# Attention's output products as three matmuls of 64 columns into one set of bank columns, instead of 128 and 64 columns and a sum

## The chip, the cores and the metric

The kernel runs on one core of a Trainium2 chip. The core has a matrix engine (TensorE, called PE in the rows), a vector engine (VectorE, DVE), an activation engine (ScalarE, ACT), a general engine (GpSimd, POOL) and a queue for transfers (SyncE, SP). PE reads its operands from on-chip memory and writes into eight accumulation banks of 512 float32 columns by 128 partitions, from which DVE and ACT read. The metric is the device time of one execution in microseconds; a number for a kernel is the median of its runs.

## What is computed

The reference is two layers of a backbone over 1024 latent tokens and 256 context tokens with 1024 features: normalise and modulate, one input projection, four parallel branches, an output projection and a gated residual. Two of the four branches are attention, over all keys (type C) and over a window (type D), and for both the part that matters here is

```
s = jnp.einsum('bgrid,bgjd->bgrij', q_blk, k, preferred_element_type=jnp.float32) * ATTN_SCALE
p = jax.nn.softmax(s, axis=-1).astype(v.dtype)
return jnp.einsum('bgrij,bgjd->bgrid', p, v)
```

with heads of 64 features, two heads of queries for each head of keys and values, and blocks of 128 query rows. The last line, probabilities times values, is what the change rewrites.

## The kernel before

Float32 products are made out of shorter numbers. For the projections (`unit_a` L429 and `unit_b` L443) a weight and an activation are each split in a high and a low part and three of the four cross products are summed in a bank. For attention, probabilities and values are split into float16 high and low parts: H and L of the probabilities P, transposed by DMA into one tile PT that holds all high tiles and then all low ones, and `vh`, whose columns 0 to 63 hold the high values of a head and 64 to 127 the low ones.

A job of attention is a block of 128 query rows with one head of type C over its ten key tiles, or two heads of type D over up to five each. It runs through a chain of steps: `scores` (PE fills up to three banks S, L974), `largest` (DVE finds the row maxima and copies S into P, L993 to L1006), `exp` (ACT, L1015), `high` (ACT makes H, L1023), `low` (DVE and POOL make L, L1032; both are transposed by DMA into PT), `values` (PE, L1045, into a bank O), `out` (ACT copies the first 64 columns of each head from O into M, L1057) and `add` (DVE adds the other 64 columns to M, L1061, and gives the bank O back). When all jobs of a chunk have been added, `norm` divides M by the sums, `turn` transposes it on PE and `gate` (DVE, L1090) multiplies with the gate.

In `values` each key tile of a head has a product of the high probabilities with all 128 columns of `vh`, and one of the low probabilities with its first 64 columns. So the bank's first 64 columns get two of the three cross products and its second 64 the third, which is why a sum of two parts follows.

The order on every engine is written by a planner at build time. It keeps a rough clock of each engine: a matmul of n columns of float16 is put down as the larger of 30 and 0.425 n ns, an operation of DVE as 130 + 1.2 n ns. Steps of jobs are queued with the time at which they are due, and `hook`, which is called between the matmuls of the projections, runs those that are due. A new job's scores are started when fewer than three jobs are in flight, enough of the six banks of tag `pm` (S, O and other small results share them) are free, and DVE and ACT are not too far behind. At the end of a group that needs the memory of attention the planner lets PE stand until the jobs are through.

Of the kernel before, what the change touches and what calls it, by code (L numbers as in the profile page):

```python
# [16 lines left out]
AF = mybir.ActivationFunctionType  # L17
# [173 lines left out]
class Program:  # L191
# [766 lines left out]
    def scores(self, typ, p, qk, vh, inv, t, t0, n, box, heads, keys, masks):  # L958
        V, S, G, T, SP = self.V, self.S, self.G, self.T, self.SP
        l, lc, nk = self.l, self.lc[self.l], len(keys)  # L960
        nh, ws, w = len(heads), 128 * nk, 128 * nk * len(heads)
        cols = [(s, kt) for s in range(nh) for kt in keys]
# [3 lines left out]
        for s in range(nh):  # L966
            i = 0
            while i < nk:
                o, m = s * nk + i, 1
                while i + m < nk and keys[i + m] == keys[i] + m and (o + m) % 4:  # L970
                    m += 1
                for b in (2, 3):
                    c = 128 * (o % 4)
# [52 lines left out]
        def low(P, H, L):  # L1026

            pt = self.tile(self.ap, (128, 20, 128), F16, "PT", "PT")
            SP.dma_start_transpose(out=pt[:, 0:w // 128, :], in_=H[:, 0:w])
            c = w * LOWS // 8  # L1030
            for E, a, b in ((V, 0, c), (G, c, w)):
                E.tensor_sub(L[:, a:b], P[:, a:b], H[:, a:b])  # L1032
            self.done(P)
            self.flight -= 1
            SP.dma_start_transpose(out=pt[:, w // 128:w // 64, :], in_=L[:, 0:w])
            self.done(H, L)
            self.pe(lambda: values(pt), "pm", lambda: vh() is not None)

        def values(pt):
            O = self.pm("O")  # L1040
            for j, (s, kt) in enumerate(cols):
                for pl in range(2):

                    m = 128 - 64 * pl
                    T.matmul(O[:, 128 * s:128 * s + m], pt[:, pl * len(cols) + j, :], vh()[:, kt, 0:m],  # L1045
                             start=(j % nk == 0 and pl == 0), stop=(j % nk == nk - 1 and pl == 1))
            self.done(pt)
            box["over"]("values")
            self.later(lambda: out(O), "", lambda: "M" in box or self.has("M"))

        def out(O):
            if "M" not in box:
                box["M"] = self.tile(self.gp, (128, 512), F32, "M", "M")
            M, c = box["M"], 128 * (t - t0) + 64 * heads[0]
            ov = O[:, :128 * nh].rearrange("p (h s d) -> p h s d", h=nh, s=2)
            mv = M[:, c:c + 64 * nh].rearrange("p (h d) -> p h d", h=nh)
            S.activation(mv, ov[:, :, 0, :], AF.Copy)  # L1057
            self.later(lambda: add(M, mv, ov, O))

        def add(M, mv, ov, O):  # L1060
            V.tensor_add(mv, mv, ov[:, :, 1, :])  # L1061
            self.done(O)
            box["left"] -= 1
            if box["left"] == 0:
                gi = 0 if typ == "C" else 1
                self.later(lambda: norm(M, gi), "gd smv", lambda: ("silu", l, gi, p, t0) in self.made)

        def norm(M, gi):
            gt = self.gd(n="gt")
            SP.dma_start(out=gt[:, :128 * n], in_=self.sgd[l][gi, p, :, 128 * t0:128 * (t0 + n)])  # L1070
            sv, rs = box["sum"], self.sm("v", "rs")
            if typ == "D":
                V.tensor_add(rs[:, 8:8 + 2 * n], sv[:, 0:2 * n], sv[:, 8:8 + 2 * n])
                V.reciprocal(rs[:, 0:2 * n], rs[:, 8:8 + 2 * n])
            else:
                V.reciprocal(rs[:, 0:2 * n], sv[:, 0:2 * n])
            m3 = M[:, :128 * n].rearrange("p (t d) -> p t d", d=64)
            self.e("msum").tensor_mul(m3, m3, rs[:, 0:2 * n].unsqueeze(2).to_broadcast([128, 2 * n, 64]))
            self.done(sv, rs)
            self.pe(lambda: turn(M, gt))  # L1080
# [714 lines left out]
```

## Time and profile before

| | |
|---|---|
| median of 3 runs | 1315.66 us (1308.14 to 1317.33) |
| the profiled execution | 1318.18 us |
| its span, first to last instruction | 1316.4 us |
| mean granted clock of TensorE | 0.987 |
| PE busy | 1272.4 us (97%) |
| DVE busy | 841.8 us (64%) |
| ACT busy | 703.4 us (53%) |
| POOL busy | 610.6 us (46%) |

Times in the rows are microseconds from the first instruction unless they are marked ns. L1045 is line 1045 of the kernel, `O<-vh,PT` means that O is written from vh and PT, and x20 that twenty instructions stand in the row. PEld is the loading of weights into the matrix engine, which can run beside its matmuls. A busy share of PE near one does not say that PE is at its peak: each matmul's recorded length contains a latency that overlaps the next one's, so the pitch at which matmuls start says more than their lengths. In the chain of work that ended last, a row is a start, a length and the work of that stretch. In the timeline, a row is a start, the time from the first start to the last end, and the instructions; in brackets stands for how long the engine had been idle before, and what it waited for. In the table by stage a row is a stretch, its length, and each engine's busy time in it, then the granted clock (1.00 is 2.4 GHz, 0.50 is 1.2 GHz), the share of DMA and GB/s.

### The profile page before, as it was taken

The numbers are of one execution on the slowest core, as the hardware profiler recorded it, in microseconds if no ns is written. First come the engines' busy times: TensorE is split into PE (matmuls) and PEld (weight loads), VectorE is DVE, ScalarE is ACT, GpSimd is POOL, SyncE is SP. The second block draws the span as 40 slices with busy tenths as digits, with TensorE's granted clock in tenths as the row PEclk, the third lists the DMA queues.
The fourth block names the chain that finished last, engine by engine and source line by source line (L and its number), as shares of the span: only waits on it lengthen the run. The fifth ranks groups of instructions, "written<-read, shape, count | busy, mean of one in ns | idle before, by whom it ended". The sixth has DMA issues, their size and how long they took to land.

```text
span 1316.4 us, 27946 instructions
## 1 busy us (share of the span) xinstructions
PE 1272.4 (97%) x10720; PEld 1121.9 (85%) x10720; DVE 841.8 (64%) x2022; ACT 703.4 (53%) x1467; POOL 610.6 (46%) x616
## 2 busy tenths in 40 slices
PE   6989999999999899999999999999999889999998
PEld 4877878889989788888999978789888778888998
DVE  4765878888897734237225957778898884523522
ACT  3555768777776831235224647667778674213210
POOL 2585855835843213234112486769486422323320
PEclk9999999999999999999999999999999999988999
DMA  9426899799789922163612257997988985105531
GB/s 365 151 77 153 136 203 214 145 201 204 146 164 192 213 75 69 45 190 115 216 33 99 90 142 145 193 196 134 189 170 156 198 162 117 40 21 196 181 112 49
DMA packets 373351, 194.13 MB, mean 147 GB/s; under 512 B 303297, under 2 KB 333665, under 8 KB 372193
## 3 DMA queue, kind: packets, MB, share of 16 engines
q1 hardware_dynamic: 373072, 192.28, 62.6%
q8 instruction: 84, 1.38, 0.4%
q14 instruction: 51, 0.41, 0.1%
q10 hardware_dynamic: 144, 0.07, 0.0%
HBM read 94.63 MB, written 23.74 MB: 90 GB/s over the span
## 4 chain that ended last, share of the span: by engine, by line
PE 79%; DVE 9%; POOL 3%; ACT 3%; issue 3%; DMA 3%; SPq 1%; POOLq 0%; ACTq 0%; DVEq 0%
PE ua L429 32%; PE ub L443 26%; PE S L974 6%; PE O L1045 5%; DVE P L993 2%; PE y L1418 2%; PE y L1414 2%; PE mod L520 1%; POOL rr L567 1%; DMA xt<-in_x 1%; PE u L1714 1%; PE kvp L1330 1%; PE sc L1386 1%; DVE qr L827 1%; DVE L L1032 1%
## 5 line engine op out<-in xcount | busy, mean ns | idle before, releaser
L429 PE MATMUL ua<-w,HT 128*128 128x256 f32 x4128 | 525.2, 285 | 0.4 <-ACT vt L1275 0.4
L429 PEld LDWEIGHTS ua<-w,HT 128*128 128x128 f32 x4128 | 502.8, 191 | 3.8 <-issue 1.7
L443 PE MATMUL ub<-HT,w 128*128 128x512 f32 (+1 forms) x1824 | 402.8, 374 | 4.8 <-ACT kT L1293 2.5
L443 PEld LDWEIGHTS ub<-HT,w 128*128 128x128 f32 x1824 | 311.7, 193 | 63.3 <-ACT kT L1293 3.3
L372 POOL TENSOR_TENSOR w<-raw,w 128x512 fp32r<-128x512 f32 x132 | 185.1, 1413 | 269.3 <-ACT w L370 240.2
L1032 DVE TENSOR_TENSOR L<-P,H 128x1120 f16<-128x1120 f32 (+2 forms) x104 | 143.1, 1376 | 18.2 <-ACT H L1023 16.8
L370 ACT ACTIVATE w<-raw 128x512 fp32r<-128x512 f32 x136 | 83.3, 625 | 109.1 <-PE ua L429 49.2
L993 DVE CUSTOM_DVE_ANT_0 P<-S,zero 128x512 f32<-128x512 f32 (+2 forms) x216 | 116.1, 581 | 29.7 <-PE S L974 14.0
L974 PE MATMUL S<-qkt 128*128 128x256 f16 (+2 forms) x768 | 124.7, 304 | 4.1 <-DVE mx L993 4.1
L1032 POOL TENSOR_TENSOR L<-P,H 128x160 f16<-128x160 f32 (+2 forms) x104 | 81.3, 782 | 97.2 <-ACT H L1023 65.0
L1023 ACT ACTIVATE H<-P 128x1280 f16<-128x1280 f32 (+2 forms) x104 | 124.5, 1197 | 2.1 <-DMA PT<-H 1.2
L1015 ACT ACTIVATE P<-P,mx,gmxC 128x1280 f32<-128x1280 f32 (+1 forms) x72 | 97.5, 1354 | 17.7 <-DVE mx L1002 16.6
L1045 PE MATMUL O<-vh,PT 128*128 128x128 f16 (+1 forms) x1952 | 101.8, 207 | 4.3 <-DVE M L1061 3.1
L974 PEld LDWEIGHTS <-qkt 128*128 128x128 f16 x768 | 64.5, 98 | 45.5 <-issue 7.6
L1045 PEld LDWEIGHTS <-PT 128*128 128x128 f16 x1952 | 88.2, 98 | 14.4 <-issue 8.0
L1598 DVE TENSOR_TENSOR tm<-ua,gb 128x512 f32<-128x512 f32 (+1 forms) x37 | 24.9, 674 | 114.5 <-PE ua L429 114.5
L573 ACT ACTIVATE ev<-ub 128x512 f32<-128x512 f32 (+1 forms) x64 | 34.7, 542 | 110.0 <-PE ub L443 89.7
L567 POOL TENSOR_TENSOR rr<-rt,mhalf 128x6 f32<-128x6 f32 (+3 forms) x60 | 76.2, 1269 | 5.0
L1015 ACT ACTIVATE P<-P,mx,gmxD 128x640 f32<-128x640 f32 (+2 forms) x72 | 61.4, 853 | 16.9 <-DVE mx L1006 12.5
L1121 DVE SCALAR_TENSOR_TENSOR sl<-th,ev 128x512 f32<-128x512 f32 (+1 forms) x40 | 34.4, 860 | 34.5 <-ACT th L1116 32.9
L993 DVE CUSTOM_DVE_ANT_0 P<-S,mask 128x512 f32<-128x512 f32 (+2 forms) x112 | 50.5, 483 | 8.1 <-PE S L974 5.4
L827 POOL TENSOR_TENSOR rt<-sw,cst 128x192 f32<-128x192 f32 x64 | 49.2, 789 | 3.0 <-ACT sw L833 2.6
(177 smaller groups left out, 1547.0 us busy)
## 6 DMA issues: line engine op xcount, KB each, us to landing
raw<-in_win SPq DMA_DIRECT2D x104, 256.0 KB
raw<-in_wmod SPq DMA_DIRECT2D x64, 256.0 KB
wm<-in_wmod SPq DMA_DIRECT2D x8, 1024.0 KB
raw<-in_wout SPq DMA_DIRECT2D x32, 256.0 KB
xt<-in_x SPq DMA_DIRECT2D x4, 1024.0 KB
silu<-sl SPq DMA_DIRECT2D x16, 256.0 KB
gt<-silu SPq DMA_DIRECT2D x16, 256.0 KB
mxd<-mg SPq DMA_DIRECT2D x16, 256.0 KB
```

The costliest lines, as they stand in the source:

```text
L370: self.S.activation(w[:, :, 0, :], rv, AF.Copy)
L372: self.e(f"w{'i' if o < 0 else 'to'[o > 0]}low{q}").tensor_sub(w[:, :, 1, :], rv, w[:, :, 0, :].bitcast(F32))
L429: self.T.matmul(ps[:, 256 * i:256 * i + 256], self.HT[:, 2 * pair + i, k, sa, :], W[k // 2][:, k % 2, sb, :], start=(j == 0 and n == 0), s ...
L443: self.T.matmul(ps[:, :128 * n], W[k // 2][:, k % 2, sa, 128 * b:128 * b + 128], self.HT[:, t0:t0 + n, k, sb, :], start=(k == 0 and m == 0 ...
L567: self.G.tensor_tensor(r[:, :n], t[:, :n], self.mhalf[:, :n], ALU.pow)
L827: E.tensor_mul(out[:, :, :, 32 * c:32 * c + 32], x[:, :, :, 32 * c:32 * c + 32], t.to_broadcast([128, 2, 3, 32]))
L974: T.matmul(sp[o // 4][:, c:c + 128 * m], qk[:, t, heads[s], :], qk[:, keys[i]:keys[i] + m, b, :], start=(b == 2), stop=(b == 3))
L993: V.tensor_tensor_reduce(out=P[:, 128 * o:128 * (o + m)], in0=sp[o // 4][:, c:c + 128 * m], in1=mk, scale=1.0, scalar=-3e38, op0=ALU.add, ...
L1015: S.activation(P[:, ws * s:ws * s + ws], P[:, ws * s:ws * s + ws], AF.Exp, scale=lc["c"][typ][0], bias=mx[:, s:s + 1], accum_out=sv[:, col ...
L1023: S.activation(H[:, 0:w], P[:, 0:w], AF.Copy)
L1032: E.tensor_sub(L[:, a:b], P[:, a:b], H[:, a:b])
L1045: T.matmul(O[:, 128 * s:128 * s + m], pt[:, pl * len(cols) + j, :], vh()[:, kt, 0:m], start=(j % nk == 0 and pl == 0), stop=(j % nk == nk ...
```

## The change

`values` makes the three cross products as three matmuls of 64 columns. All three go into the same 64 columns of the bank, so the bank sums them. The high probabilities are the weights of the first two, which read the high and the low values; the low probabilities are those of the third. A weight load stands ahead of every matmul, before and now. `out` copies the finished columns, 64 for each head and next to each other, and gives the bank back. The step `add` with its instruction of DVE is gone, and what it did besides (it counts the jobs that are left and starts `norm`) is now done by `out`.

```
-                for pl in range(2):
-
-                    m = 128 - 64 * pl
-                    T.matmul(O[:, 128 * s:128 * s + m], pt[:, pl * len(cols) + j, :], vh()[:, kt, 0:m],
-                             start=(j % nk == 0 and pl == 0), stop=(j % nk == nk - 1 and pl == 1))
+
+                for pl, pv in ((0, 0), (0, 1), (1, 0)):
+                    T.matmul(O[:, 64 * s:64 * s + 64], pt[:, pl * len(cols) + j, :], vh()[:, kt, 64 * pv:64 * pv + 64],
+                             start=(j % nk == 0 and pl + pv == 0), stop=(j % nk == nk - 1 and pl == 1))
...
-            ov = O[:, :128 * nh].rearrange("p (h s d) -> p h s d", h=nh, s=2)
-            mv = M[:, c:c + 64 * nh].rearrange("p (h d) -> p h d", h=nh)
-            S.activation(mv, ov[:, :, 0, :], AF.Copy)
-            self.later(lambda: add(M, mv, ov, O))
-
-        def add(M, mv, ov, O):
-            V.tensor_add(mv, mv, ov[:, :, 1, :])
+            S.activation(M[:, c:c + 64 * nh], O[:, :64 * nh], AF.Copy)
             self.done(O)
```

The planner's clocks see other lengths, so it deals the rows of attention out anew. On PE, the start of the first output block was this before (ua is a projection's bank, O_1536 the output bank):

```order
L429 MATMUL ua_1475<-w_1207,HT 128x256 x6
L1045 LDWEIGHTS PT_1404
L1045 MATMUL O_1536<-vh_993,PT_1404 128x128
L1045 LDWEIGHTS PT_1404
L1045 MATMUL O_1536<-vh_993,PT_1404 128x64
```

and is this now, where the matmul stands on line 1044:

```order
L429 MATMUL ua_1475<-w_1207,HT 128x256 x6
L1044 LDWEIGHTS PT_1404
L1044 MATMUL O_1536<-vh_993,PT_1404 128x64
L1044 LDWEIGHTS PT_1404
L1044 MATMUL O_1536<-vh_993,PT_1404 128x64
L1044 LDWEIGHTS PT_1404
L1044 MATMUL O_1536<-vh_993,PT_1404 128x64
```

A key tile's two loads and two matmuls have become three and three; the program has 976 more of each on PE.

On DVE, late in the second layer's attention, the row of the maxima of one job (L1006) was followed by an add and the next subtraction before:

```order
L1006 TENSOR_SCALAR mx_14617<-mx_14617 128x2
L1061 TENSOR_TENSOR M_14370<-M_14370,O_14577 128x128
L1032 TENSOR_TENSOR L_14635<-P_14499,H_14634 128x1120
L1073 TENSOR_TENSOR rs_14676<-sum_14145 128x8
L1074 RECIPROCAL rs_14676<-rs_14676 128x8
L703 TENSOR_SCALAR tb_14683<-tab_14594,lconst_9554 128x128
```

and is now followed by the reciprocals of a chunk that is complete, and then the subtraction:

```order
L1006 TENSOR_SCALAR mx_15430<-mx_15430 128x2
L1066 TENSOR_TENSOR rs_15453<-sum_14928 128x8
L1067 RECIPROCAL rs_15453<-rs_15453 128x8
L1032 TENSOR_TENSOR L_15449<-P_15309,H_15448 128x1120
L703 TENSOR_SCALAR tb_15509<-tab_15426,lconst_10002 128x128
```

The add has left DVE's queue there, as it has in 104 places, and the reciprocals moved ahead of the subtraction.

On PE, shortly behind that place, two pieces of a projection (ub) stood ahead of two jobs' scores in a row before; the rows are the end of the projection, and the start of the first job's scores:

```order
L579 MATMUL mt_14812<-cst,M_14370 128x128 x4
L443 MATMUL ub_14774<-HT,w_14014 128x256 x6
L443 MATMUL ub_14774<-HT,w_14570 128x256 x6
L974 LDWEIGHTS qkt_13547
L974 MATMUL S_14852<-qkt_13547 128x256
```

Now one job's scores stand ahead of those two pieces, and the other's behind them; the rows are the end of the first job's scores, the projection, and the start of the second job's:

```order
L974 LDWEIGHTS qkt_14238
L974 MATMUL S_15653<-qkt_14238 128x256
L443 MATMUL ub_15592<-HT,w_14646 128x256 x6
L443 MATMUL ub_15592<-HT,w_15382 128x256 x6
L974 LDWEIGHTS qkt_14238
L974 MATMUL S_15703<-qkt_14238 128x256
```

One of the two jobs moved ahead of 12 matmuls of the projection.

## Rows read from the trace of the kernel before

**Rows 1.** The page: busy time, share of the span, instructions of PE and DVE

```profile
PE 1272.4 (97%) x10720; PEld 1121.9 (85%) x10720; DVE 841.8 (64%) x2022; ACT 703.4 (53%) x1467; POOL 610.6 (46%) x616
```

**Rows 2.** The page: the chain that ended last, shares of the span by engine

```profile
PE 79%; DVE 9%; POOL 3%; ACT 3%; issue 3%; DMA 3%; SPq 1%; POOLq 0%; ACTq 0%; DVEq 0%
```

**Rows 3.** Busy time by stage: the two layers' attention

```profile
90.00:500.00 410.00, 400.92 (x3675) 348.08 (x3674) 316.59 (x858) 279.22 (x571) 217.47 (x229) 0.99 0.84 168
...
800.00:1110.00 310.00, 300.00 (x2765) 260.45 (x2763) 249.09 (x677) 222.22 (x434) 180.23 (x185) 0.99 0.86 167
```

**Rows 4.** Groups by line and form: products and adds (busy us, mean ns; idle before)

```profile
L1045 PE MATMUL O<-vh,PT 128*128 128x128 f16 x976 | 98.6, 221 | 3.7 <-DVE M L1061 3.1 <-DVE mx L993 0.6
L1045 PE MATMUL O<-vh,PT 128*128 128x64 f16 x976 | 94.5, 193 | 0.6 <-DMA PT<-L 0.5
...
L1061 DVE TENSOR_TENSOR M<-M,O 128x64 f32<-128x64 f32 x64 | 13.4, 210 | 1.4 <-ACT M L1057 1.3
...
L1061 DVE TENSOR_TENSOR M<-M,O 128x128 f32<-128x128 f32 x40 | 11.1, 280 | 19.1 <-ACT M L1057 19.1
```

**Rows 5.** Timeline of PE and PEld, one output block and what follows it

```profile
154.22 1.02 PE L1045 MATMUL O<-vh,PT 128*128 128x128 f16 x20
...
154.22 0.88 PEld L1045 LDWEIGHTS <-PT 128*128 128x128 f16 x20
...
155.06 0.19 PE L1045 MATMUL O<-vh,PT 128*128 128x64 f16 x1
155.08 0.38 PE L974 MATMUL S<-qkt 128*128 128x512 f16 x1
```

**Rows 6.** The chain from 150 to 165 us: an output and a score block

```profile
154.38 0.87 PE O L1045 x20
155.25 1.08 PE S L974 x6
```

**Rows 7.** The bank O: idle time before its instructions until (us, times)

```profile
  ACT M L1057: 20.4, 12
  DVE M L1061: 3.1, 2
```

**Rows 8.** Timeline of ACT, then of DVE, in stretch B

```profile
1029.43 0.45 ACT L1057 ACTIVATE M<-O 128x128 f32<-128x128 f32 x2 [0.36 <-POOL ge L1250]
...
1031.04 1.33 DVE L1032 TENSOR_TENSOR L<-P,H 128x1120 f16<-128x1120 f32 x1
1032.28 0.48 DVE L1061 TENSOR_TENSOR M<-M,O 128x128 f32<-128x128 f32 x2
```

**Rows 9.** Timeline of PE: a wait in B, a projection ahead of C

```profile
1032.61 1.01 PE L1045 MATMUL O<-vh,PT 128*128 128x128 f16 x20 [1.64 <-DVE M L1061]
...
1070.93 1.68 PE L443 MATMUL ub<-HT,w 128*128 128x256 f32 x12
```

**Rows 10.** The chain by stretches: first and last of ten adds

```profile
248.04 0.21 DVE M L1061
...
1074.14 0.27 DVE M L1061
```

**Rows 11.** Busy time by stage (PE, PEld, DVE, ACT, POOL), granted clock: B, C, A

```profile
1028.00:1039.20 11.20, 6.35 (x83) 4.91 (x80) 10.57 (x39) 7.98 (x19) 2.33 (x4) 1.00 1.00 198
1075.00:1083.00 8.00, 4.55 (x41) 2.87 (x40) 7.47 (x29) 5.13 (x14) 1.28 (x3) 0.78 0.64 129
436.00:448.10 12.10, 7.73 (x102) 5.88 (x99) 10.75 (x41) 10.89 (x26) 2.64 (x5) 1.00 0.95 217
448.10:451.50 3.40, 3.38 (x10) 2.71 (x11) 3.11 (x11) 2.48 (x8) 0.32 (x1) 0.50 0.92 201
1079.50:1086.40 6.90, 5.75 (x25) 3.59 (x25) 6.10 (x26) 4.29 (x11) 0.48 (x1) 0.51 0.76 143
```

**Rows 12.** One line's instructions: durations ns, first and last start us

```profile
L1330 PE MATMUL kvp<-vt,kf x32: 222/222/270, 479.2 to 480.1; 128*64 128x64 f32 x32
```

## The prediction

> **What bounds the kernel now.** I read the page's totals first: PE is busy 1272.4 of 1316.4 us, DVE 841.8 [rows 1]. The chain that ended last says the same: 79% of it is PE work and 9% DVE [rows 2]. So a change here is worth what it does to PE: how long its instructions take, and how long PE stands. PE stands 44.0 us in all. The table by stage shows how much of it lies in the two layers' attention: 9.1 us from 90 to 500 and 10.0 us from 800 to 1110 [rows 3]. Only these 19.1 us can be touched through attention's DVE work.
>
> Within attention the standing is not spread out. Much of it lies in three short stretches, in which score blocks and output blocks follow each other on PE with hardly any projection between. A is 436 to 448 us, where PE is busy 7.73 of 12.1 us; B is 1028 to 1039, 6.35 of 11.2; C is 1075 to 1083, 4.55 of 8.0 [rows 11]. That is 4.4, 4.85 and 3.45 us of standing, together 12.7. DVE is busy 10.75, 10.57 and 7.47 us in them: there DVE sets the pace, elsewhere PE does.
>
> **The change, part by part.**
>
> *Products on PE.* There are 976 key tiles (128 keys for one head), each with one matmul of 128 and one of 64 columns [rows 4]. After it each has three of 64. The columns stay 192 per tile; one matmul and one weight load per tile are added, 976 of each. The recorded means, 221 and 193 ns, overlap each other and are no price. The price is the pitch: 20 matmuls start at 154.22 and the next block at 155.08, so 0.86 us for ten tiles, 86 ns a tile [rows 5]. If a matmul costs a fixed part f and c per column, two kinds of block in the chain give both: a score block, 2560 columns in six matmuls, takes 1.08 us; an output block, 1920 columns in twenty, 0.87 [rows 6]. Three quarters of the first, 0.81 us, is 1920 c + 4.5 f. The difference to 0.86 or 0.87 is 15.5 f, so f is 3.2 to 3.9 ns, and 976 added matmuls cost 3.1 to 3.8 us. That is the upper end by this form of matmul. The lower end is nothing: a fixed part below zero makes no sense, so three of 64 do not undercut 128 + 64. Between them lie two nearer rows. The last 64-column product of a block starts at 155.06 and the next matmul, which has a weight load of its own, at 155.08: 20 to 30 ns with the rounding [rows 5]. And the retention's 32 short matmuls with their loads start between 479.2 and 480.1, 29 ns apart [rows 12]; 3 x 29 is 87 ns a tile, 1 us in all. I take 2.0 us, between these and the solved value. What hides the third weight load is the matmul before it: 20 loads lie in the same 0.88 us as 20 products [rows 5], those behind a 64-column matmul too. Without that cover it is the third rival.
>
> A rule speaks against this part. The Trainium skill, page "TensorE: Matmul & The Clock Gate", section "Back-to-back issue gap", holds that in a stream of pairs of weight load and matmul both set the spacing, about 81 ns a matmul at 128 columns. By that figure, as an estimate, 976 more pairs would cost some 79 us and the time would be near 1395 us. The row here has 43 ns a pair in the mean, so the trace does not agree, and the sum goes by the row.
>
> *DVE's sum.* 104 adds go, 64 of 210 ns and 40 of 280 ns, together 24.6 us of DVE [rows 4]. DVE also stood 20.4 us in 12 places because the add at the head of its queue waited for ACT's copy [rows 7]; queued behind it stand the maxima of the next scores, for which PE waits only when it has no projection to run. Nearly all of that lies beside PE work. What lay on the path are the pieces of the chain that are adds: I count ten of 0.05 us or more, the first at 248.04 and the last at 1074.14, sum 1.75 us [rows 10]. So -1.8 us; at least nothing, at most all of the 12.7 us.
>
> *The bank.* O's bank is now given back by ACT's copy, not by DVE's add. PE waited for an add twice, 3.1 us in all [rows 7]. The longer one is in B: ACT's copies had ended at 1029.88, the adds stood behind the subtraction L and ended at 1032.76 [rows 8], and PE's block had stood 1.64 us [rows 9]. Such waits go. But DVE is busy nearly throughout B, and what ends there is the scores' maxima and exponentials: PE would stand a little later instead. I take 0 of the 3.1 us, and keep both ends.
>
> *ACT.* The copy reads 64 or 128 columns that lie together instead of every other half; as many elements, one instruction as before. 0.
>
> *The order.* The scheduler now sees matmuls of another length, no add, and earlier banks, so most rows of attention are dealt out anew. A, B and C remain: as many score blocks are bunched in A and B as before, and the last excerpt of the change shows one block of C pulled ahead of 12 projection matmuls, which are worth up to 1.7 us [rows 9]. DVE was at other work then, so I take half, -0.8 us. Ahead of the first output product nothing moves, and next to nothing from 500 to 800 and after 1110 us.
>
> **Sum.** +2.0 - 1.8 - 0.8 = -0.6 us on the profiled execution's 1318.18 us (its span of 1316.4 and 1.8 around it). That execution lies 2.5 us above the median of the runs shown, 1315.66, so the change should come out at 1315.1: nothing that can be measured.
>
> **The rivals.**
> 1. *DVE's relief goes further.* If the freed 24.6 us let DVE keep ahead, the 12.7 us of standing go. So does what the clock loses: behind A and at the end of C the granted clock was 0.50 and 0.51, its 1.2 GHz level, with PE busy 3.38 and 5.75 us [rows 11], which is half of that lost, 4.6 us. At most 17.3 us: 1298; half of it, 1307. For it: DVE was busy almost throughout A, B and C. Against: the adds in B are three, some 0.8 of DVE's 10.6 us, and the bunched score blocks are still there.
> 2. *The new order is worse.* Another stretch like these costs 3.5 to 4.9 us of standing and, as behind A and C, 1.7 to 2.9 us of slower clock: about 1321 with one, 1328 with two. For it: the order is dealt out anew by a planner that knows none of these times. Against: the bunches stand at the same places as before.
> 3. *Slower: narrow matmuls wait for their weights.* If pairs of load and 64-column matmul could not follow each other every 29 ns, the loads would set the block. The mean pitch of 43 ns is the upper bound: 129 - 86 = 43 ns a tile, 42 us, 1357 us; the middle, 36 ns, gives 22 ns a tile, 21 us, 1337. It turns to slower from 33 ns on, since 13.2 us over 976 tiles are 13.5 ns a tile. For it: no row shows two 64-column products of this kind in a row, and the load before a 64-column matmul has now always been hidden behind one of 128. Against: behind each 64-column product the next load and matmul followed in 20 to 30 ns.
>
> The rule of 81 ns, which I quoted above from the Trainium skill, would be this third rival at its worst; the row of 43 ns excludes it, and I give it 0.01 of the third rival's chance.
>
> **How the numbers follow.** The forecast has 0.67, rival 1 0.14 with half of it beyond 1%, rival 2 0.11, rival 3 0.08. One per cent, 13.2 us, is about what a measurement of this kernel can tell from no change. Below 1302.5 lies half of rival 1: 0.07 faster. Above 1328.8 lies rival 3 and the far end of rival 2: 0.09 slower. The rest, 0.84, is the same. The range from 1303 to 1325 leaves out these and a little more of rival 2, 0.19 in all.
>
> **What would show it.** In the profile after: one form of output product, 64 columns, x2928; an output block of 30 of them in 0.86 to 0.90 us (1.08 with rival 3 at 36 ns); no add by DVE, and DVE near 817 us; no output product that waits for DVE's M, at most for ACT's; A, B and C at about the same places, and PE standing 40 to 45 us in all. I am wrong if PE stands under 35 us (rival 1), if new idle stretches or more slow clock appear outside A, B and C (rival 2), or if the blocks take over 1 us (rival 3).

## The result, and the profile after

The changed kernel takes 1327.42 us (median; 1324.84 to 1329.82), the kernel before 1316.49 beside it: ratio 1.0091, 95% interval 1.0064 to 1.0119. The change costs some 11 to 12 us. It was forecast at 1315.1 with a range up to 1325, so the time lies outside the range. The case that was given most, no change within 1%, holds by the ratio alone, and only just; the loss is real.

The page of the changed kernel, its busy row, answers to [rows 1]; the second line is the mean granted clock of its one core.

```profile
PE 1273.3 (96%) x11696; PEld 1122.4 (85%) x11696; DVE 821.4 (62%) x1918; ACT 703.1 (53%) x1467; POOL 617.5 (47%) x616
...
core 0: 1322.1 us, clock 0.988
```

This execution took 1324.84 us, the fastest of these four. PE has 976 matmuls more and is busy 0.9 us longer; DVE has lost the 104 adds and 20.4 us. PE stands 48.8 us (1322.1 less 1273.3) against 44.0. The chain of waits of this page leads back over 8% of the span only, so nothing below rests on it.

The output products, by line and form [rows 4]; then a timeline of PE, one block of 30 of them and what follows [rows 5]:

```profile
L1044 PE MATMUL O<-vh,PT 128*128 128x64 f16 x2928 | 105.7, 194 | 12.1 <-DMA PT<-L 6.2 <-DVE mx L993 3.0 <-DMA PT<-H 2.4
```

```profile
165.32 1.05 PE L1044 MATMUL O<-vh,PT 128*128 128x64 f16 x30
166.20 1.03 PE L974 MATMUL S<-qkt 128*128 128x512 f16 x4
```

The block takes 0.88 us to the next start, before 0.86. But PE now stands 12.1 us ahead of output products, before 4.3 (3.7 and 0.6 in [rows 4]). What it waits for, PE's waits after (us in total, times, longest):

```profile
PE O L1044 <- DMA PT<-L: 6.2, 8, 1.4
...
PE O L1044 <- DVE mx L993: 3.0, 2, 2.3
...
PE S L974 <- DVE mx L993: 2.9, 5, 1.2
...
PE O L1044 <- DMA PT<-H: 2.4, 1, 2.4
```

PT is the transposed probabilities, in two parts from H and L, brought by transfers. No product waits for DVE's M any longer [rows 7]. The stages answer to [rows 3] (PE, PEld, DVE, ACT, POOL busy, granted clock):

```profile
90.00:500.00 410.00, 400.54 (x4167) 347.71 (x4167) 300.44 (x797) 278.27 (x571) 220.53 (x229) 0.99 0.84 168
500.00:800.00 300.00, 298.46 (x2192) 272.54 (x2191) 141.56 (x249) 108.28 (x273) 107.04 (x106) 0.98 0.34 110
800.00:1110.00 310.00, 297.96 (x3218) 258.88 (x3217) 247.53 (x632) 224.94 (x436) 184.40 (x186) 1.00 0.89 169
```

PE stands 9.5 us in the first layer's attention (before 9.1) and 12.0 in the second's (10.0). The table by stretches shows A, B and C at their old times, each with what came behind it [rows 11]:

```profile
436.00:448.10 12.10, 8.96 (x118) 6.10 (x115) 8.89 (x32) 9.94 (x25) 3.59 (x3) 1.00 1.16 248
448.10:454.90 6.80, 5.49 (x41) 4.19 (x41) 6.41 (x17) 6.45 (x17) 3.50 (x4) 0.50 0.85 172
1028.00:1039.20 11.20, 10.89 (x118) 10.22 (x117) 6.79 (x25) 6.26 (x12) 8.78 (x8) 1.00 0.90 167
1039.20:1042.00 2.80, 1.84 (x38) 1.51 (x38) 2.73 (x6) 2.13 (x6) 0.00 (x0) 1.00 1.08 228
1075.00:1083.00 8.00, 8.00 (x110) 7.88 (x109) 7.07 (x22) 6.31 (x16) 1.49 (x2) 1.00 1.10 187
1086.40:1093.00 6.60, 3.65 (x51) 2.77 (x50) 6.02 (x18) 5.97 (x16) 1.50 (x3) 1.00 0.70 133
```

In the old windows of A, B and C the standing fell from 12.7 us to 3.45 (3.14, 0.31 and 0), but 5.2 us stand just behind them (1.31, 0.96 and 2.95), where there was next to none before. So A kept its standing (4.37 us before, 4.45 now), C lost little of it and comes later, and only B gave up most of its 4.85. Together it is 8.7 us for 12.7. In the rest of attention the standing doubled, from 6.4 us (9.1 and 10.0 less 12.7) to 12.8 (9.5 and 12.0 less 8.7). Some of it lies at places that had none before. One of these, PE's timeline at 302 us (from 299.5 to 304.6 us PE stands 1.37 us, and did not stand there before):

```profile
302.13 0.23 PE L1044 MATMUL O<-vh,PT 128*128 128x64 f16 x2
303.74 0.99 PE L1044 MATMUL O<-vh,PT 128*128 128x64 f16 x28 [1.37 <-DMA PT<-L]
```

Two products of the block run on the part from H; the other 28 wait for the part from L.

**A bookkeeping that the experiments use.** Span times one minus the mean clock is what the slower clock takes from PE, if PE is busy at these times ("lost"). The clock is given to 0.001, so that lost is good to some 0.7 us. In the profile before, lost is 17.1 us, and PE's busy time without it 1255.3; after, 15.9 and 1257.4. So a span is three things: some 1255 to 1258 us of work at the 2.4 GHz level, the standing, and the lost time. For the timed runs, where only span and clock are known, span less lost ("rest") is work plus standing. Before ran again beside each set of experiments. Medians over the runs:

| kernel | time, us | ratio to before [95%] | rest | lost |
|---|---|---|---|---|
| before (sets of 9 to 35 runs) | 1314.5 to 1316.4 | 1 | 1300.8 to 1301.7 | 10.5 to 14.4 |
| the change (4 runs) | 1327.42 | 1.0091 [1.0064, 1.0119] | 1309.2 | 16.6 |
| the change again (6) | 1328.30 | 1.0088 [1.0060, 1.0116] | 1307.2 | 17.9 |
| change, order of before (12) | 1313.49 | 0.9979 [0.9967, 0.9990] | 1300.6 | 10.5 |
| before, narrow products only (12) | 1315.48 | 0.9998 [0.9980, 1.0016] | 1301.1 | 11.8 |

It is rough: from run to run of one kernel a microsecond lost lengthens the span by about 0.7 (all kernels here together), as some of it is taken where PE would have stood a little later.

### The profile page after: what moved, and what is told of

The parts are those of the page before. It is cut to its first block, busy times and chain, and to the rows that moved or that the text cites. A ratio compares the mean times of both kernels' runs of the same rounds, so it can differ in the third digit from the quotient of the medians.

```text
span 1322.1 us, 29793 instructions
## 1 busy us (share of the span) xinstructions
PE 1273.3 (96%) x11696; PEld 1122.4 (85%) x11696; DVE 821.4 (62%) x1918; ACT 703.1 (53%) x1467; POOL 617.5 (47%) x616
## 5 line engine op out<-in xcount | busy, mean ns | idle before, releaser
L372 POOL TENSOR_TENSOR w<-raw,w 128x512 fp32r<-128x512 f32 x132 | 188.7, 1440 | 247.4 <-ACT w L370 231.9
L1032 DVE TENSOR_TENSOR L<-P,H 128x1120 f16<-128x1120 f32 (+2 forms) x104 | 146.8, 1411 | 27.9 <-ACT H L1023 27.2
L1032 POOL TENSOR_TENSOR L<-P,H 128x160 f16<-128x160 f32 (+2 forms) x104 | 89.3, 860 | 98.2 <-ACT H L1023 60.2
L1044 PE MATMUL O<-vh,PT 128*128 128x64 f16 x2928 | 105.7, 194 | 12.1 <-DMA PT<-L 6.2
L1044 PEld LDWEIGHTS <-PT 128*128 128x128 f16 x2928 | 94.3, 98 | 23.4 <-issue 9.5
```

The lines of the kernel that those rows point to most:

```text
L372: self.e(f"w{'i' if o < 0 else 'to'[o > 0]}low{q}").tensor_sub(w[:, :, 1, :], rv, w[:, :, 0, :].bitcast(F32))
L1044: T.matmul(O[:, 64 * s:64 * s + 64], pt[:, pl * len(cols) + j, :], vh()[:, kt, 64 * pv:64 * pv + 64], start=(j % nk == 0 and pl + pv == 0) ...
```

## The experiments

**e1_old_order: the change's instructions in the order of before.** The planner goes on counting what it counted before: the old price of a tile's products, and an add of DVE that is not there. On every engine the instructions stand in the order of before, but for products and adds; the traces of the two agree in that.

```diff
-            return max(30.0, 0.425 * n)
+            return 84.4 / 3 if n == 64 else max(30.0, 0.425 * n)
...
+            end = self.free["DVE"] = t + 130 + 1.2 * n
...
+            self.later(lambda: add(M, mv, O))
+
+        def add(M, mv, O):
+            self.clock.ghost = (M.tensor.name, O.tensor.name, 64 * nh)
             self.done(O)
```

> The change's instructions (three products of 64 columns, no add) in the order of the kernel before: the planner still counts the add's time on DVE and in the bank, though no such instruction is issued, and counts each 64-column product at a third of the old pair. On every engine the rows then stand as before, but for the products and the missing adds. Theory 'order' (the loss comes from the rows that were dealt out anew, the new instructions cost nothing): the time is that of the kernel before or 1 to 4 us under it, 1312 to 1317 us, and PE waits for the transposed probabilities stay near 0.5 us. Rival 'instructions' (narrow products, or the missing add by itself, cost the time): 1325 to 1330 us, as the changed kernel.

Measured 1313.49 us over 12 runs, 0.9979 [0.9967, 0.9990]: 2.9 us faster than before, and 1.1% under the change (0.9979 over 1.0091). The instructions are the same in this run and in the change; only where they stand differs. So the whole loss, and more, is the order. The rows of this kernel, page and core, then PE's waits (L1060 is the change's L1044):

```profile
PE 1265.0 (96%) x11696; PEld 1117.4 (85%) x11696; DVE 827.3 (63%) x1918; ACT 702.9 (54%) x1467; POOL 611.5 (47%) x616
...
core 0: 1311.6 us, clock 0.995
```

```profile
PE O L1060 <- DMA PT<-L: 5.6, 7, 1.5
```

Here too products wait 5.6 us for the part from L, where 0.5 was expected, and PE stands 46.6 us: these waits alone are not what makes the change slow. In the profiled executions the two orders differ by 2.2 us of standing (48.8, 46.6) and 9.3 us of lost time (15.9, 6.6); in the medians of the table by 7 to 9 us of rest and 6 to 7 us lost.

Stretch A shows that equal standing can come with an unequal clock. PE after, then PE in this experiment:

```profile
438.28 2.94 PE L520 MATMUL mod<-raw,cond 128*32 128x256 f32 x16 [0.38 <-DVE mx L993]
441.15 2.14 PE L974 MATMUL S<-qkt 128*128 128x256 f16 x20
...
443.89 1.03 PE L1044 MATMUL O<-vh,PT 128*128 128x64 f16 x30 [0.25 <-DVE mt L542]
444.90 0.60 PE L974 MATMUL S<-qkt 128*128 128x256 f16 x4
447.87 0.23 PE L1044 MATMUL O<-vh,PT 128*128 128x64 f16 x2 [2.37 <-DMA PT<-H]
448.94 1.67 PE L1044 MATMUL O<-vh,PT 128*128 128x64 f16 x28 [0.84 <-DMA PT<-L]
450.43 1.04 PE L974 MATMUL S<-qkt 128*128 128x256 f16 x4
451.94 2.92 PE L443 MATMUL ub<-HT,w 128*128 128x512 f32 x6 [0.47 <-ACT kT L1286]
```

```profile
439.00 1.04 PE L991 MATMUL S<-qkt 128*128 128x256 f16 x8
441.76 0.68 PE L537 MATMUL mod<-raw,cond 128*32 128x256 f32 x4 [1.72 <-DVE mx L1010]
...
446.16 1.04 PE L1060 MATMUL O<-vh,PT 128*128 128x64 f16 x30
447.03 0.60 PE L991 MATMUL S<-qkt 128*128 128x256 f16 x4
449.02 1.66 PE L460 MATMUL ub<-HT,w 128*128 128x512 f32 x6 [1.38 <-ACT kT L1307]
```

In the new order the sixteen matmuls of the modulation (mod) stand ahead of a score block of twenty instead of behind the scores, and an output block stands 2.37 and 0.84 us for its probabilities. The old order stands elsewhere: 1.72 us ahead of mod and 1.38 ahead of the projection ub. In sum PE stands 4.45 us from 436 to 454.9 after and 4.25 in the experiment, but ub starts at 451.94, not 449.02. The granted clock is 0.50 for the 6.8 us from 448.1 on (above), and the six matmuls of ub take 2.92 us where they took 1.66; before it was 0.50 there for 3.4 us [rows 11]. In the experiment it stays at full speed (busy time by stretches):

```profile
436.00:448.10 12.10, 8.77 (x124) 6.23 (x119) 10.03 (x37) 10.01 (x24) 2.47 (x4) 1.00 1.09 217
448.10:454.90 6.80, 5.88 (x56) 5.04 (x57) 3.62 (x13) 5.59 (x14) 3.39 (x3) 1.00 1.06 214
```

**b_narrow: the narrow products alone.** Before's order and DVE's add; each half of the bank keeps its columns.

```diff
-                    T.matmul(O[:, 128 * s:128 * s + m], pt[:, pl * len(cols) + j, :], vh()[:, kt, 0:m],
+                for pl, pv in ((0, 0), (0, 1), (1, 0)):
+                    T.matmul(O[:, 128 * s + 64 * pv:128 * s + 64 * pv + 64], pt[:, pl * len(cols) + j, :], vh()[:, kt, 64 * pv:64 * pv + 64],
```

> Only the products change: three of 64 columns for each key tile, but into the two halves of the bank as before, and DVE's add stays. The planner counts the three as the old two, so every engine's order is that of the kernel before. What it tells is the price of narrow products alone. The prediction took +2.0 us, from 0 to 3.8 (1316 to 1320 us). If the first 30-product block is 0.86 us long, nothing: 1314 to 1318 us. If narrow products were the cause of the loss: 1325 us or more.

Measured 1315.48 us, 0.9998 [0.9980, 1.0016]: the narrow products cost at most 2 us of time. Between this kernel and the one above lie 0.2%, some 2.5 us. That is what goes with the add, the bank's halves and the copy's form, all three together, and the two intervals overlap, so it is not clear of noise.

**a_late15: output blocks later.** A second theory was that the planner, which gives a transfer too little, now deals output blocks out before their probabilities are there, and that this is what costs. The step is put 1.5 us later in the planner's time (SAFE are the 300 ns that it had):

```diff
-            self.pe(lambda: values(pt), "pm", lambda: vh() is not None)
+            self.later(lambda: values(pt), "pm", lambda: vh() is not None, SAFE + 1500.0, True)
```

> The changed kernel, with the planner told to put each output block 1.5 us later in its own time than before, so that a projection's matmuls stand ahead of it. Theory 'late probabilities' (PE stands 8.6 us inside or ahead of output blocks until the transposes of L and H have landed, and that is the loss): those waits fall under 2 us and the time under 1320 us. Rival 'draw' (the whole order is dealt anew, some good, some bad, and these waits are only what this draw shows): the waits may fall, but the time stays within 1320 to 1332 us, since other waits take their place.

Measured 1315.19 us, 0.9987 [0.9974, 1.0000]. No product waits for PT any more, and the loss is gone. The rival's range, 1320 to 1332 us, was missed. That would do for the theory, had the next runs not followed.

**a_sem60, b_sem60: another order with no meaning.** The planner puts 80 ns between an instruction and the one that waits for it. With 60 it deals all rows out anew, for the change (a) and for before (b):

```diff
-                end += 80
+                end += 60
```

> The changed kernel with the same number of the planner at 60 instead of 80 ns. Theory 'draw': anywhere from 1306 to 1330 us, and its distance to the kernel before with 60 ns is not again +11 us but between -10 and +10. Rival 'the change's own order is worse': 1324 to 1331 us, as the changed kernel.

> The kernel before, all its instructions the same, with one number of the planner changed that has nothing to do with the products: it counts 60 ns instead of 80 from the end of a producer to its consumer. The order of attention is dealt out anew. Theory 'draw' (any new order moves the time by up to 10 us either way): 1306 to 1330 us, more than 4 us away from 1316 in one of these variants at least. Rival 'the change's own order is worse' (the order that follows from the missing add is worse for a reason): the kernel before stays at 1312 to 1319 us.

Measured 1316.82 us for the change, 0.9992 [0.9976, 1.0009], and 1321.34 for before, 1.0033 [1.0020, 1.0046]. A number that says nothing of output blocks takes the change's loss away as well as the 1.5 us did, and costs the kernel before 0.3%.

**after_again, a_sem100, b_sem100.** The change once more, unedited; and 100 in the place of 60.

> The changed kernel itself, once more and on the chip of this set, beside the kernel before. Its earlier four runs were 1324.8 to 1329.8 us. If the loss is the kernel's and not that chip's: 1323 to 1330 us, 1.006 to 1.012 of the kernel before. If it was the chip or the hour: under 1320 us.

> The changed kernel, the planner counting 100 ns instead of 80 from a producer's end to its consumer: another order of attention, the same instructions. Theory 'draw': anywhere from 1308 to 1330 us. Rival 'the change's own order is worse for a reason': 1322 us or more, as the changed kernel; the variant with 60 ns, at 1316.8 us, spoke against it already.

> The kernel before with the same number of the planner at 100 ns. Theory 'draw': anywhere from 1308 to 1330 us; the variant with 60 ns came to 1321.3. Rival (the old order is a good one that only the change lost): 1317 to 1325 us here too, never under the kernel before.

Measured 1328.30 us, 1.0088 [1.0060, 1.0116], for the change: its loss repeats. Its page and core:

```profile
PE 1280.8 (96%) x11696; PEld 1127.6 (85%) x11696; DVE 822.4 (62%) x1918; ACT 703.5 (53%) x1467; POOL 618.3 (47%) x616
...
core 0: 1328.1 us, clock 0.983
```

Of its 11.7 us over the profile before, 3.3 are standing (47.3, 44.0) and 8.4 busy time, of which 5.5 lie in the clock (22.6 lost, 17.1). With 100 the change takes 1333.62 us, 1.0138 [1.0112, 1.0165], and before 1324.29, 1.0083 [1.0060, 1.0107]. So both kernels can be had 0.8 to 1.4% slower than before's order has them, without one instruction more or less. (The five runs of before with 100 spread from 1313 to 1328 us, so its 0.8% is rough.)

**a_sem100_late15, b_late15, e1_late15, a_late30: the remedy elsewhere.** If late probabilities were the cause, the 1.5 us would help wherever products wait; put with the 100, on before, on the first experiment, and doubled (3000.0 for 1500.0):

> The worst order so far (the changed kernel with 100 ns in the planner, 1333.6 us), with the output blocks put 1.5 us later in the planner's time. Theory 'late probabilities': its 10.7 us of PE's waits for transposes fall under 3 us and the time by 8 us or more, to 1326 us or less, as the same step took the changed kernel from 1328 to 1315. Rival 'draw' (1315 was a lucky order): the waits fall but the time lies anywhere from 1312 to 1334 us.

> The kernel before with its output blocks put 1.5 us later. It has only 0.5 us of waits for transposes, so theory 'late probabilities' has nothing to give it: 1313 to 1320 us if the new order is as good. Rival 'draw': anywhere from 1310 to 1330 us.

> The change's instructions with the planner still counting the add (the order that gave 1313.5 us), and output blocks 1.5 us later. That run had 5.6 us of PE's waits for transposes; theory 'late probabilities' takes 3 to 5 us off: 1308 to 1311 us, the fastest of all. Rival 'draw': 1311 to 1328 us.

> The changed kernel with output blocks 3.0 us later instead of 1.5. Theory 'late probabilities': the waits are gone at 1.5 us already, so nothing more is gained and jobs end later: 1314 to 1322 us. Rival 'draw': anywhere from 1310 to 1334 us.

Measured 1337.36 us (1.0171 [1.0126, 1.0215]), 1343.06 (1.0208 [1.0165, 1.0251]), 1340.30 (1.0196 [1.0169, 1.0224]) and 1329.93 (1.0115 [1.0089, 1.0142]): slower than before in all four. The waits for the transposed probabilities did fall where they had been long, from 10.7 to 1.2 us with the 100 and from 5.6 to 1.3 on the first experiment, and the time did not fall with them: 1333.6 became 1337.4, not clear of noise, and 1313.5 became 1340.3. So late probabilities by themselves are not the cause. Later output blocks are no remedy, and that a_late15 lost nothing belongs to its own order. But the rival 'draw' allowed at most 1334, 1330 and 1328 us for the first three, and they lie above: whether putting output blocks later also costs by itself, these runs don't show. Two of the four have one order: b_late15 and e1_late15 differ in products and adds alone, and there too the change's instructions are 2.8 us ahead (1340.30, 1343.06; the intervals overlap). PE's waits of b_late15 show what it gets instead:

```profile
PE O L1045 <- DVE mx L993: 6.0, 4, 4.1
PE ua L429 <- POOL w L372: 5.3, 1, 5.3
PE mt L579 <- POOL M L1078: 4.5, 2, 3.6
```

In the profile before the first of these was 0.6 us, and the other two do not occur. This kernel stands 58.6 us in its profile and has 30.8 us lost in the median.

**h_old0, h_old1: which layer.** The change, with the planner counting the old way in the attention of the first layer alone (h_old0), or of the second alone (h_old1):

```diff
+            if l == 0:
+                self.later(lambda: add(M, mv, O))
+            else:
+                add(M, mv, O)
```

> The change's instructions; the planner counts as before (the add's time, the old price of the products) in the first layer's attention and as changed in the second's. Through the first layer every engine's order is that of the kernel before. With the old order in both layers the time was 1313.5 us, with the new one in both 1328. In the changed kernel's trace 5 us are lost by 451 us and 5 more by 1076 us. If the loss sits in the orders of both layers by halves: 1318 to 1323 us, with the first 451 us as in the kernel before. If all of it comes from the first layer: 1312 to 1316. If from the second: 1325 or more.

> The other half: the planner counts as changed in the first layer's attention and as before in the second's. Through the first layer every engine's order is that of the changed kernel, so the end of its attention should again come about 5 us later than in the kernel before, with PE's waits for transposes at 302 and 446 us. The second layer's order is a new one. By halves: 1317 to 1325 us. If the first layer's order costs nothing: 1312 to 1316.

Measured 1320.51 us, 1.0039 [1.0013, 1.0065], and 1320.07, 1.0029 [1.0011, 1.0048]. The four combinations are all there: in its second layer every engine's order in h_old0 is that of the changed kernel, and in h_old1 that of before, not a new one as was expected. Over the first experiment that is +7.0 for the new order in the second layer and +6.6 for it in the first, each to some 3 or 4 us; the sum, 13.6, is about what both together cost (13.9 and 14.8). So no one bad place makes the loss: about half of it comes with each layer's order. The stages between and behind, h_old0 first, then h_old1 (columns as in the stages above):

```profile
500.00:800.00 300.00, 298.49 (x2237) 272.73 (x2236) 143.77 (x258) 112.88 (x283) 109.79 (x108) 0.99 0.36 113
800.00:1110.00 310.00, 297.46 (x3168) 258.02 (x3168) 242.22 (x616) 219.69 (x425) 180.95 (x184) 0.98 0.86 167
```

```profile
500.00:800.00 300.00, 298.44 (x2197) 272.58 (x2199) 141.52 (x252) 109.06 (x276) 107.01 (x107) 0.98 0.35 110
800.00:1110.00 310.00, 302.41 (x3268) 262.67 (x3269) 244.51 (x629) 224.35 (x435) 182.05 (x187) 1.00 0.88 170
```

With the second layer's new order PE stands 12.5 us in that layer's attention, with the old one 7.6. The first layer's new order shows less in its own attention than behind it: the last output product of that layer starts at 473.1 us in h_old1 (472.1 to 473.7 in the three profiles with this order) and at 470.1 to 472.4 in the four with the old one, not 5 us later as was expected, but the clock between the layers is lower. Which placements within a layer carry the loss was not separated further, and stays open.

## Why the prediction was right or wrong

*Products: right.* Predicted +2.0 us, between 0 and 3.8. Over the 88 full blocks of the trace, first start to next start, the median is 859 ns before and 884 after: 25 ns for ten added pairs of load and matmul, 2.5 ns each, 2.4 us in all. The solved value of f, 3.2 to 3.9 ns, was a little high; it compared blocks of unlike kinds, which may be why. The Trainium skill, page "TensorE: Matmul & The Clock Gate", section "Wait — 56ns, not 53.3ns?", gives a matmul at the upper level N / 2.4 GHz and about 2.5 ns; as an estimate, 976 more matmuls are 2.4 us. The trace agrees. The third rival, loads that set the pace, is out: 884 ns over 30 is 29.5 ns a pair. The Trainium skill, same page, section "Back-to-back issue gap", has 81 ns a matmul at 128 columns for such a stream; pairs of 128 and 64 columns in turn took 43 ns in the mean, so the trace does not agree.

*DVE's sum and the bank: the sign is right, the mechanism is not shown.* Predicted -1.8 and 0 us, with the products +0.2 without the order. In the order of before, the whole change gives -2.9 us (-4.3 to -1.3), so the forecast of this part lies outside the interval, by 3 us in the middle. It was to come from a shorter standing of PE. But by the bookkeeping rest is the same, 1300.6 and 1300.8 us beside each other, and lost fell from 14.4 to 10.5; in the profiles PE even stands longer, 46.6 us for 44.0. So the gain shows as clock and not as standing; why is open, and before's own lost varies as much between sets (10.5 to 14.4). No more came of DVE's 20 us, so the first rival is out as well: the 3.1 us of waits for the add are gone, and the waits for the part from L grew from 0.5 to 5.6, much as the prediction had it for the bank, where PE would stand a little later instead.

*The order: this step failed.* The prediction put it at -0.8 us: A, B and C remain, one block of C is pulled ahead, little else matters. It measured +13.9 to +14.8 us (the change against its own instructions in the old order). Two things were wrong in the step. First, it looked for the effect in the three stretches where PE stood before. There, with what moved just behind them, the new order did better than forecast, 12.7 us down to 8.7; the cost came in the rest of attention (6.4 us more), such as at 302 us, where PE had not stood before, and in the clock. Second, it took the dealing-out anew for neutral where no row showed a loss. The draws show how far it is from that: before's instructions took 1316, 1321, 1324 and 1343 us in four orders, the change's 1313, 1315, 1317, 1328, 1330, 1334, 1337 and 1340 in eight (the mixed orders of the two layers left out). 1313 is the order of before, and 1340 that of 1343, so beside before's there are nine orders: two cost nothing and seven cost 0.3 to 2.1%. Three of the four with another order by 60 or 100 ns alone are among the seven. The order of before is among the best here, so most others lose.

The second rival, a worse new order, is what happened; 0.11 was too little. The time it gave for two more bad stretches, 1328 us, is what was measured, but that is in part luck: no two stretches make it. By the medians of the timed runs about half of the loss is standing and half the clock; the single profiled executions divide it in other ways: of 10.5 us over the first experiment 2.2 are standing, of 5.7 over before 4.8 are. It is spread over both layers.

*The marks.* As forecast: one form of product x2928, a block of 0.86 to 0.90 us, DVE near 817 (821.4), no wait for M. Not as forecast: B, of which little stayed, and 48.8 us of standing for 40 to 45; the prediction named new idle stretches outside A, B and C as the sign that the second rival holds, and they are there.

**A version that beats both**: the change's instructions in the order of before, 1313.49 us, 0.2% (0.1 to 0.3) under before and 1.1% under the change.

## What to carry over

Where a planner writes the order, a change of instructions is two changes: measure the new instructions in the old order first, then ask what the new order does. In this kernel, whose PE is busy 97% of its span, seven of nine other orders lost time; so where the order is already that good, price a dealing-out anew as a likely loss with a wide range, not as zero, and do not look for it only where PE stood before. And one run in which a remedy works proves little as long as any edit that draws the order anew moves the time as much; try the remedy on a second order.

## What the runs showed of the hardware

The granted clock also fell where PE had not been standing. The table by stretches of the changed kernel:

```profile
454.90:512.90 58.00, 58.00 (x584) 48.58 (x584) 25.99 (x78) 20.92 (x53) 13.21 (x13) 1.00 0.35 82
512.90:516.30 3.40, 3.40 (x16) 2.80 (x15) 1.07 (x2) 0.66 (x2) 0.89 (x2) 0.51 0.13 39
```

PE was busy all of 58.00 us, and then ran 3.4 us at the 1.2 GHz level, with 16 matmuls. In the profile before the same 3.4 us had 1.00. And behind 8.77 us busy of 12.1 in stretch A the clock stayed up in the first experiment, while behind 8.96 of 12.1 it fell in the change. So the standing just ahead does not alone decide where the clock falls; what does, these runs don't show.

The clock costs outside attention too. From the start of the last output product of the first layer to the first score of the second the trace after takes 321.8 us, the first experiment 319.3, though the order hardly differs there; the clock does (after above, 0.98). It goes with the order of the first layer's attention: in the three profiles with the new one this stretch takes 321.4 to 321.8 us at a clock of 0.98, in the four with the old one 317.9 to 319.3 at 0.99. The stage in the first experiment:

```profile
500.00:800.00 300.00, 298.51 (x2220) 272.78 (x2219) 142.28 (x251) 111.56 (x279) 110.03 (x109) 0.99 0.35 110
```

Between orders, the median of the time lost ran from 10.5 to 30.8 us; for the kernel before alone it ran from 10.5 to 14.4 between sets.
